# Second feed-forward product begun without its residual, another order in the first quad, and the last weight splits on VectorE

## The chip, the cores and the metric

One core of a Trainium2 chip runs the whole program once. The metric is the device time of one execution in microseconds. The kernel before took 1949.84 us as the median of three runs (1946.95 to 1949.94). The profile is of one more execution, of 1947.49 us, whose span from the first to the last instruction is 1945.7 us.

TensorE multiplies (PE in the profile; PEld is its weight loading), VectorE is DVE, ScalarE is ACT, GpSimd is POOL. Transfers are issued from the queue of SyncE (SP) or of ScalarE (ACTq).

## The reference, cut to what matters

One layer of an encoder on 1024 new frames and 64 frames of a running stream, model width 1024, all in float32. Only its last two lines are touched here:

```
x1 = layer_norm(ALPHA * x + merged @ w_out, ln1_g, ln1_b)
ff = jnp.square(jax.nn.relu(x1 @ w_ff1)) @ w_ff2          # w_ff1: 1024 x 4096, w_ff2: 4096 x 1024
x2 = layer_norm(ALPHA * x1 + ff, ln2_g, ln2_b)
```

`ALPHA * x1` is the residual of the second product.

## The kernel before

**Precision.** Each float32 factor is split in a high and a low part, both stored as float32r: ScalarE copies (`split`, L357), VectorE subtracts (L360). A product is three matmuls, high by high, high by low, low by high (`mm3`, L349, L352, L353).

**Layout.** Activations lie transposed, features on the partitions and the 1088 frames along the free axis, up to the last stage. Until the feed-forward part they lie in three chunks of 384, 384 and 320 frames (`CHUNKS`).

**Units.** Up to the feed-forward part, work comes as units: 128 columns of a weight against one chunk each, 24 matmuls a chunk (`product`, `unit`). A queue of jobs sets their order. Each job loads the weight piece after the next (`wload`, two buffers `wr`) and splits the next one (`wsplit`, two buffers `wh`/`wl`). Work on VectorE and ScalarE for the next stage is written as generators that go one step on at each unit (`BG`, `slot`).

**Opening of the feed-forward part** (`open_ff`, `first_units`). The last 512 of the 4096 hidden columns are four units with relu and square after them (`post_h`), stored in `hidD`. They bridge the layer norm of the third chunk: u0, u1 and u2 run on chunk 0 and 1 while chunk 2 is normalised, then u0 and u1 on chunk 2, then the rest of u2, then u3 on chunks 0, 1, 2. Meanwhile `spill_x1` writes `x1` (high, low and whole: `x1Dh`, `x1Dl`, `y1D`) to memory, and `x1_sums` computes sums of quarters of `x1` (t1 to t4), over the first two chunks in two pieces of 192 frames, each with two tiles of the two `wr` buffers. The third chunk's sums come in `ff_first`.

**Quads.** The other 3584 hidden columns are done as 2 by 2 blocks with seven instead of eight products (`stream`). A quad is seven steps P1 to P7, over 256 columns of the result and all 1088 frames. The order of the steps is P6, P1, P7, P5, P4, P2, P3, where P6, P7, P4 are of the quad before; the first quad has P1, P5, P2, P3 alone. `USES` says which weight sum and which operand sum a step needs, `BANK` which PSUM tile it adds to: P1, P6, P7, P4 add up in bank tile a (two buffers), P5 and P3 in b, P2 in c. After each step `done` reads the banks, so P6 of a quad has to wait until P1 has been read. `between` is called after each step and issues what comes next.

- `ff_first`: 14 quads of 24 matmuls a step. Operands `xb` are loaded from `x1Dh` and `x1Dl` into the buffers that the chunks of `x1` held, once these are done with; weights come through one `raw` buffer (`load_raw`), their sums are split in `produce` (`wv`). `done` makes the hidden layer and its sums and stores them in `hvD`, 14 writes a quad.
- `ff_second`: 7 blocks of 4 quads, 12 matmuls a step. Operands `hv` of even blocks come into the big buffers that `xb` held (`load_even`, into `BIG`), of odd blocks into a pool of their own (`load_odd`). Weights: `load_w`, two buffers `wr`, and `split_w` into parts a, b, c (`wac`, `wb`); `next_w(q + 3)` after P4 of quad q. Results add up in SBUF in four tiles `YF[0..3]` (`yf`), one for each quad of a block. At the start of `ff_second` they are loaded from `y1D`, two on ACTq and two on SP, so the residual is in them from the start; the first accumulation in block 0 multiplies by `ALPHA` (L1307), the others add (L1309). Each step's result goes to one half of a tile, 128x544.
- Pools on one stack take the place of the closed ones: in `ff_second` first `wr2`, then `wvb` (for `wb`), then `y2p` (for `yf`), then `hvp1`. A new tile waits for the last use of what lay there.

**The end.** The 512 hidden columns of the four units are the last factor of the second product. In block 6 `last_weight(k)` (after P2 of quads 24 to 27) loads and splits 128 rows of `w_ff2`, and `last_hidden(k)` 128 rows of `hidD`; their low parts are computed on GpSimd (`low=G`). `last_ff2` then goes through nine tiles of 128 frames: `turn` transposes `yf` (8 transposes, read by ScalarE), `last_products` multiplies, VectorE adds (L1418), and a layer norm follows. From the second tile on all PSUM tiles come from one pool of eight banks.

`tc.issue_after(x)` keeps what its block traces behind instruction x on x's engine.

Of the kernel before, what the change touches and what calls it, by code (L numbers as in the profile page):

```python
# [9 lines left out]
F32 = mybir.dt.float32  # L10
# [7 lines left out]
D = 1024  # L18
# [3 lines left out]
P = 128  # L22
# [29 lines left out]
def hybrid_layer(ctx, tc, x_prompt, x_sample, cache_conv, state_C, state_n, state_m, w_in, b_gate,  # L52
# [50 lines left out]
    def J(ap, fn, kind="w"):  # L103
        jobs.append((ap, fn, kind, stage[0]))
# [823 lines left out]
    def x1_sums():  # L928
        tv = pools["tv"] = pool("tv", 1, stack=ff1)
        for nm in ("t1", "t2", "t3", "t4"):  # L930
            XV[nm] = [tv.tile([P, 4, HT2], F32R, tag=nm + e, name="x" + nm + e) for e in "hl"]

        for o in (0, 192):
            yield from sums(o, 192, 0, o, 1, o)

    def sums(a, n, ca, oa, cb, ob):
        b11, b21 = (Y2[ca][:, kh:KT:2, oa:oa + n] for kh in range(2))
        b12, b22 = (Y2[cb][:, kh:KT:2, ob:ob + n] for kh in range(2))
        z = [wpool.tile([P, KT * P], F32, tag="wr", name="xs")[:, :4 * n].rearrange("p (k t) -> p k t", t=n) for _ in range(2)]

        def keep(nm, src):
            split(*(t[:, :, a:a + n] for t in XV[nm]), src)
        V.tensor_tensor(z[0], b11, b12, ALU.subtract)
        keep("t1", z[0])
        yield
        V.scalar_tensor_tensor(z[1], z[0], -1.0, b22, ALU.mult, ALU.subtract)
        keep("t2", z[1])
        yield
        V.tensor_tensor(z[0], b22, b12, ALU.subtract)
        keep("t3", z[0])  # L950
        V.scalar_tensor_tensor(z[1], z[1], -1.0, b21, ALU.mult, ALU.subtract)
        keep("t4", z[1])
        yield

    def first_units(u, hi, lo):
        post = post_h(u)
        unit(hi, lo, post, (0,))
        held.append((hi, lo, post))
        if u == 1:
            third = 2 + next(i for i, p in enumerate(pieces) if p[3] == 1)  # L960
            w3 = pools["rawp"].tile([P, 2 * KT * P], F32R, tag="raw", name="w3")
            h3, l3 = w3[:, 0:KT * P], w3[:, KT * P:]
            split(h3, l3, raws[third])
            his[third] = tuple(t.rearrange("p (k n) -> p k n", n=P) for t in (h3, l3))
            early[0] = product(*his[third], 0)
            for h in held:
                unit(*h, (1,))
            early[1] = product(*his[third], 1)
            drain("misc")
            for ci in range(3):  # L970
                spill_x1(ci)
            BG["misc"].append(x1_sums())
            step("misc")
            for h in held:
                unit(*h, (2,))

    N(open_ff)
    for u in range(4):
        c0 = (4 * KT - 4 + u) * P
        if u < 2:  # L980
            J(wcols(w_ff1[0], c0), lambda hi, lo, u=u: first_units(u, hi, lo), "f" if u else "w")
        else:
            add_unit(w_ff1[0], c0, post_h(u))

    def stream(n, weight, operand, nk, done, between=None):

        bank = {}

        def run(q, nm):
            an, bn = USES[nm]  # L990
            bk = BANK[nm]
            if nm in ("P1", "P2", "P5"):
                bank[q, bk] = pools["psy" + bk].tile([P, 2, 512], F32, tag=bk, name="y" + bk)
            ps = bank[q, bk]
            for sg in range(2):
                for k in range(nk):
                    bh, bl = operand(q, bn, k, slice(sg * HB, (sg + 1) * HB))
                    mm3(ps[:, sg, :HB], *weight(q, an, k), bh, bl, nm in ("P1", "P2", "P5") and k == 0, k == nk - 1, more=True)
            done(q, nm, {k: bank.get((q, k)) for k in "abc"})

        for q in range(n + 1):
            for nm in ("P6", "P1", "P7", "P5", "P4", "P2", "P3"):
                old = nm in ("P6", "P7", "P4")
                if 0 <= q - old < n:
                    run(q - old, nm)
                    if between:
                        between(q - old, nm)
# [12 lines left out]
    def ff_first():  # L1020
# [26 lines left out]
        def produce():  # L1047
            for q in range(NQ):
# [3 lines left out]
                def item(nm, src):  # L1052
# [6 lines left out]
                    slot_of[q, nm] = (hi, lo)  # L1059
                    made[0] += 1  # L1060
                item("a11", c[0, 0])
                V.tensor_tensor(c[0, 0], c[0, 0], c[1, 0], ALU.add)
                yield
                V.tensor_tensor(c[1, 0], c[1, 0], c[1, 1], ALU.add)
                item("s1", c[1, 0])
                yield
                item("a12", c[0, 1])
                yield
# [183 lines left out]

    def ff_second():
        wr2 = pools["wr2"] = pool("wr2", 2)
        wvb = pool("wvb", 3)
        yp = pool("y2p")
        odd = ExitStack()
        hvp1 = pool("hvp1", 1, stack=odd)
        banks = ExitStack()
# [39 lines left out]
        def done(q, nm, bk):  # L1299
            blk, jp = divmod(q, 4)  # L1300
            for m, b, mh, th in (("P1", "a", 0, 0), ("P5", "b", 1, 1), ("P2", "c", 0, 0), ("P6", "a", 0, 1), ("P6", "b", 0, 1),
                                 ("P7", "a", 1, 1), ("P4", "a", 1, 0)):
                if m == nm:
                    y = halves(YF[jp][:, mh, th * HT2:(th + 1) * HT2])
                    op = ALU.subtract if mh else ALU.add
                    if blk == 0 and (nm, b) in (("P1", "a"), ("P5", "b"), ("P6", "a"), ("P4", "a")):
                        V.scalar_tensor_tensor(y, y, ALPHA, cols2(bk[b]), ALU.mult, op)  # L1307
                    else:
                        V.tensor_tensor(y, y, cols2(bk[b]), op)  # L1309

        def between(q, nm):
            if (q, nm) == (1, "P5"):
                next_w(2)
            if nm == "P4":
                next_w(q + 3)
            blk, n = q // 4, len(steps)
            steps.append(nm)
# [12 lines left out]
            if nm == "P2" and blk == 6:  # L1330
                last_weight(q % 4)
            if q == nq - 1 and nm in ("P5", "P2"):
                k, pp = (2, ph) if nm == "P5" else (3, pl)
                t = pp.tile([P, 3072], F32R, tag="p", name="hid")
                last_hidden(k, t[:, 0:TW], t[:, TW:2 * TW])
# [4 lines left out]

        steps, lead = [], []

        def load_y(j, eng):
            eng.dma_start(YF[j], y1D[j * 2 * P:(j + 1) * 2 * P, :].rearrange("(b p) t -> p b t", p=P))
        load_y(0, S)
        load_w(2, S)
        load_y(1, S)
        load_w(3, S)
        load_y(2, nc.sync)
        load_y(3, nc.sync)  # L1350
        stream(nq, weight, operand, 2, done, between)
        last_ff2(YF, lead[0], banks)

    WH, WL = [], []

    def last_hidden(k, hi, lo):
        raw = pools["la"].tile([P, T], F32, tag="hidr", name="hidr")
        nc.sync.dma_start(raw, hidD[k * P:(k + 1) * P, :])
        for x in (hi, lo):
            G.memset(x[:, T:].bitcast(F32), 0.0)  # L1360
        split(hi[:, :T], lo[:, :T], raw, low=G)
        HID[k] = (hi, lo)

    def last_weight(k):
        la = pools["la"]
        raw = pools["wr2"].tile([P, KT * P], F32, tag="wr", name="wr")
        nc.sync.dma_start(raw, w_ff2[0, (28 + k) * P:(29 + k) * P, :])
        WH.append(la.tile([P, D], F32R, name=f"w2h{k}"))
        WL.append(la.tile([P, D], F32R, name=f"w2l{k}"))
        split(WH[k], WL[k], raw, low=G)  # L1370
        if k < 2:
            last_hidden(k, la.tile([P, TW], F32R, name=f"hid{k}h"), la.tile([P, TW], F32R, name=f"hid{k}l"))

    def last_products(i, hf, p, ks):
        hs = slice(hf * 512, hf * 512 + 512)
# [5 lines left out]
    def last_ff2(YF, lead, banks):  # L1381
# [6 lines left out]
        ps = [None]  # L1388

        def turn(i, banks=None):  # L1390
            n = tile_len(i)
            yt = ytp[:, i % 3 * D:(i % 3 + 1) * D]
            for kh in range(2):
                p = banks[:, kh] if banks is not None else ps[0].tile([P, 512], F32, tag="m", name="pt")
                for k in range(4):
                    j = 4 * kh + k
                    TE.transpose(p[:n, k * P:(k + 1) * P], YF[j // 2][:, j % 2, i * P:i * P + n], ident)
                S.activation(yt[:n, kh * 512:(kh + 1) * 512], p[:n], AF.Copy)
            return yt

        prev = None
        for i in range(NT):
# [6 lines left out]
            for hf in range(2):  # L1409
                hs = slice(hf * 512, hf * 512 + 512)  # L1410
                if i:
                    p = ps[0].tile([P, 512], F32, tag="m", name="po")
# [5 lines left out]
                V.tensor_tensor(y[:, hs], p[:n], y[:, hs], ALU.add)  # L1418
            if i == 0:
                banks.close()  # L1420
                ps[0] = pool("pse", 8, space=PSUM)
                nxt = turn(1)
            stats = ln_stats([y[:, 0:512], y[:, 512:1024]], n)
            if prev:
# [94 lines left out]
```

## Time and profile before

| | |
|---|---|
| median of three runs | 1949.84 us |
| the profiled execution's own time | 1947.49 us |
| its span | 1945.7 us |
| PE busy | 1888.8 us, 97% |
| DVE busy | 1411.8 us, 73% |
| ACT busy | 714.4 us, 37% |
| POOL busy | 144.4 us, 7% |
| mean granted clock of TensorE | 0.990 |

The page cuts the span in 40 slices of 48.6 us. Rows of stretches ("windows") give, for each stretch, its length, then busy time and number of instructions for PE, PEld, DVE, ACT, POOL, then the granted clock, the busy share of the DMA engines and GB/s. A row of the timeline gives start, duration, engine, line, operation, out<-in; in brackets how long the engine sat idle before and what ended it.

### The profile page before, as it was taken

How to read it: one execution, taken by the hardware profiler on the slowest of the kernel's cores; microseconds unless marked ns; L12 is line 12 of the kernel's file. 1: busy time of each engine (PE TensorE's matmuls, PEld its weight loads, DVE VectorE, ACT ScalarE, POOL GpSimd, SP SyncE). 2: the span in 40 equal slices, each digit the busy share in tenths (PEclk: the TensorE clock that was granted, in tenths of full speed). 3: DMA queues.
4: the chain of work that ended last, by engine and by line, in shares of the span. 5: the costliest groups of instructions: out<-in, count | busy, mean ns of one | idle time of the engine just before them, and what ended most of it. 6: DMA issues, size and time to landing. Idle time of an engine off the chain costs nothing.

```text
span 1945.7 us, 31671 instructions
## 1 busy us (share of the span) xinstructions
PE 1888.8 (97%) x12732; PEld 1867.9 (96%) x12732; DVE 1411.8 (73%) x2280; ACT 714.4 (37%) x1269; POOL 144.4 (7%) x237
## 2 busy tenths in 40 slices
PE   8999999999999999999999999899999959999998
PEld 7999999999999999999999999899999959999986
DVE  4957876787678867877774557687777747888856
ACT  4323322332233223323452215676666611212223
POOL 1112210001000100000000000000000000000134
PEclk9999999999999999999999999999999979999999
DMA  4121311122112211225334316856666897676322
GB/s 143 52 78 54 125 51 53 53 72 57 56 33 65 75 56 44 61 88 191 111 107 144 92 36 227 296 213 230 243 235 235 326 337 268 243 269 237 119 78 82
DMA packets 231350, 269.31 MB, mean 138 GB/s; under 512 B 13599, under 2 KB 170767, under 8 KB 231203
## 3 DMA queue, kind: packets, MB, share of 16 engines
q1 hardware_dynamic: 227299, 261.78, 40.0%
q10 hardware_dynamic: 3904, 5.51, 0.8%
q8 instruction: 100, 1.64, 0.3%
q14 instruction: 47, 0.39, 0.1%
HBM read 172.35 MB, written 94.82 MB: 137 GB/s over the span
## 4 chain that ended last, share of the span: by engine, by line
PE 91%; DVE 4%; DMA 3%; ACT 1%; issue 1%; POOL 0%; SPq 0%; ACTq 0%; DVEq 0%; POOLq 0%
PE g L349 18%; PE g L352 18%; PE g L353 18%; PE ya L349 5%; PE ya L352 5%; PE ya L353 5%; PE yb L352 3%; PE yb L353 3%; PE yb L349 3%; PE yc L352 1%; PE yc L353 1%; PE yc L349 1%; PE m L353 1%; PE m L349 1%; PE m L352 1%; PE po L353 1%
## 5 line engine op out<-in xcount | busy, mean ns | idle before, releaser
L349 PE MATMUL g<-xh,wh 128*128 128x384 f32 (+1 forms) x1920 | 634.4, 330 | 0.4 <-ACT xh L180 0.4
L352 PE MATMUL g<-xl,wh 128*128 128x384 f32 (+1 forms) x1920 | 628.3, 327 | 0.9 <-DVE xl L181 0.9
L353 PE MATMUL g<-xh,wl 128*128 128x384 f32 (+1 forms) x1920 | 628.3, 327 | 0.0
L352 PEld LDWEIGHTS g<-xl,wh 128*128 128x128 f32 x1920 | 360.7, 188 | 1.3 <-DVE xl L181 1.2
L349 PEld LDWEIGHTS g<-xh,wh 128*128 128x128 f32 x1920 | 360.6, 188 | 1.1 <-ACT xh L180 0.6
L353 PEld LDWEIGHTS g<-xh,wl 128*128 128x128 f32 x1920 | 360.3, 188 | 0.1
L593 DVE SCALAR_TENSOR_TENSOR acc<-glu,vecs,acc 128x1118 f32<-128x1118 f32 x240 | 332.5, 1385 | 3.6
L357 ACT ACTIVATE wh<-wr 128x1024 fp32r<-128x1024 f32 x83 | 87.9, 1059 | 189.3 <-PE g L352 167.9
L360 DVE TENSOR_TENSOR wl<-wr,wh 128x1024 fp32r<-128x1024 f32 x83 | 103.8, 1250 | 64.0 <-ACT wh L357 63.1
L349 PE MATMUL ya<-hv,wac 128*128 128x272 f32 x336 | 98.3, 293 | 27.9 <-DVE yf L1307 24.6
L357 ACT ACTIVATE wac<-wr 128x512 fp32r<-128x512 f32 (+1 forms) x52 | 44.0, 847 | 175.5 <-PE ya L353 90.7
L353 PE MATMUL ya<-hv,wac 128*128 128x272 f32 x336 | 98.1, 292 | 0.0
L352 PE MATMUL ya<-hv,wac 128*128 128x272 f32 x336 | 97.6, 291 | 0.0
L1309 DVE TENSOR_TENSOR yf<-yf,ya 128x544 f32<-128x544 f32 x100 | 71.7, 718 | 32.2 <-PE ya L353 32.2
L349 PEld LDWEIGHTS ya<-hv,wac 128*128 128x128 f32 x336 | 64.9, 193 | 28.6 <-DVE yf L1307 25.1
L360 DVE TENSOR_TENSOR wv<-raw,wv 128x512 fp32r<-128x512 f32 x84 | 56.5, 686 | 23.3 <-ACT wv L357 22.9
L360 DVE TENSOR_TENSOR wac<-wr,wac 128x512 fp32r<-128x512 f32 (+1 forms) x52 | 49.9, 959 | 30.7 <-ACT wac L357 30.6
L357 ACT ACTIVATE wv<-raw 128x512 fp32r<-128x512 f32 x84 | 51.2, 623 | 48.0 <-DMA raw<-in_w_ff_dram 40.0
L353 PE MATMUL yb<-hv,wac 128*128 128x272 f32 x224 | 65.7, 293 | 0.0
L349 PE MATMUL yb<-hv,wac 128*128 128x272 f32 x224 | 65.6, 293 | 0.0
L352 PE MATMUL yb<-hv,wac 128*128 128x272 f32 x224 | 65.6, 293 | 0.0
L352 PEld LDWEIGHTS ya<-hv,wac 128*128 128x128 f32 x336 | 64.4, 192 | 0.0
(410 smaller groups left out, 4318.2 us busy)
## 6 DMA issues: line engine op xcount, KB each, us to landing
hv<-hvD SPq DMA_DIRECT2D x90, 544.0 KB
wr<-in_w_in_dram SPq DMA_DIRECT2D x64, 512.0 KB
hvD<-zh SPq DMA_DIRECT2D x98, 272.0 KB
wr<-in_w_ff_dram SPq DMA_DIRECT2D x32, 512.0 KB
raw<-in_w_ff_dram SPq DMA_DIRECT2D x15, 1024.0 KB
hvD<-r SPq DMA_DIRECT2D x56, 272.0 KB
hvD<-t SPq DMA_DIRECT2D x42, 272.0 KB
hv<-hvD SPq DMA_DIRECT2D x16, 272.0 KB
```

The costliest lines, as they stand in the source:

```text
L349: first = TE.matmul(out, lh, rh, start=start, stop=False, skip_group_check=more)
L352: TE.matmul(out, lh, rl, start=False, stop=False, skip_group_check=more)
L353: TE.matmul(out, ll, rh, start=False, stop=stop, skip_group_check=more)
L357: a = S.activation(hi, src, AF.Copy)
L360: low.tensor_tensor(lo, src, hi.bitcast(F32), ALU.subtract)
L593: V.scalar_tensor_tensor(acc, glu[:, j:j + AC], vecs[:, c, j:j + 1], acc, ALU.mult, ALU.add))
L1309: V.tensor_tensor(y, y, cols2(bk[b]), op)
```

## The change

1. `x1_sums` goes over the first two chunks in three pieces of 128 frames. A piece that narrow takes one `wr` buffer for its two tiles.
2. `first_units`: all four units are handled in it. u0 on chunk 2, then the split of u3, u1 on chunk 2, u3 on chunks 0 and 1, u2 on chunk 2, u3 on chunk 2.
3. `stream`: the first quad's order becomes P1, P2, P5, P3, in both products. `produce` makes the weight part a12 of the first quad before s1.
4. `ff_second` no longer loads `yf`. In block 0 the first write to each half is a ScalarE copy (scale 1 or -1), the rest add on VectorE. `residual(q)`, after P3 of quads 4 to 9, 12 to 17 and 20 to 23, loads one of 16 pieces of `y1D` (128x544) into a spare part of `BIG[4]` or `BIG[5]`; the call after it adds ALPHA times the piece on VectorE. `y2p` is opened before `wvb`.
5. Weights: `next_w(2)` comes after P4 of quad 0, behind its evacuations, and `next_w(3)` after P3 of quad 1.
6. The last splits: loads and splits are separate, with a timetable `LAST` over quads 24 to 27; the low parts are on VectorE; `hidr` has two buffers.
7. `last_ff2`: two PSUM pools of four banks, for odd and even tiles, instead of one of eight.

```diff
-        for o in (0, 192):
-            yield from sums(o, 192, 0, o, 1, o)
+        for o in range(0, CN, P):
+            yield from sums(o, P, 0, o, 1, o)
...
-            early[0] = product(*his[third], 0)
+            ps3 = [product(*his[third], 0)]
             for h in held:
                 unit(*h, (1,))
-            early[1] = product(*his[third], 1)
+            ps3.append(product(*his[third], 1))
...
-            for h in held:
-                unit(*h, (2,))
+            unit(*held[0], (2,))
+            wsplit(third + 1)
+            for ci in range(2):
+                post_h(2)(ci, *CHUNKS[ci], ps3[ci])
+            unit(*held[1], (2,))
+            unit(*his[third + 1], post_h(3), (0, 1))
+            unit(*his[third], post_h(2), (2,))
+            unit(*his[third + 1], post_h(3), (2,))
...
-            for nm in ("P6", "P1", "P7", "P5", "P4", "P2", "P3"):
+            for nm in ("P6", "P1", "P7", "P5", "P4", "P2", "P3") if q else ("P1", "P2", "P5", "P3"):
...
         wr2 = pools["wr2"] = pool("wr2", 2)
+        yp = pool("y2p")
         wvb = pool("wvb", 3)
-        yp = pool("y2p")
...
                     if blk == 0 and (nm, b) in (("P1", "a"), ("P5", "b"), ("P6", "a"), ("P4", "a")):
-                        V.scalar_tensor_tensor(y, y, ALPHA, cols2(bk[b]), ALU.mult, op)
+                        tail["s"] = S.activation(y, cols2(bk[b]), AF.Copy, scale=-1.0 if mh else 1.0)
                     else:
-                        V.tensor_tensor(y, y, cols2(bk[b]), op)
+                        tail["v"] = V.tensor_tensor(y, y, cols2(bk[b]), ALU.subtract if mh else ALU.add)
+
+        def residual(q):
+            life, i = divmod(q - 4, 8)
+            if i - 1 in rest:
+                (j, mh, th), t = rest.pop(i - 1)
+                y = YF[j][:, mh, th * HT2:(th + 1) * HT2]
+                V.scalar_tensor_tensor(y, t, ALPHA, y, ALU.mult, ALU.add)
+            n = 6 * life + i
+            if i < 6 and n < 16:
+                j, mh, th = n // 4, n // 2 % 2, n % 2
+                t = BIG[4 + i % 2][:, 4 * HT2:5 * HT2].bitcast(F32)
+                r = (2 * j + mh) * P
+                nc.sync.dma_start(t, y1D[r:r + P, th * HT2:(th + 1) * HT2])
+                rest[i] = ((j, mh, th), t)
 
         def between(q, nm):
-            if (q, nm) == (1, "P5"):
-                next_w(2)
-            if nm == "P4":
+            if (q, nm) == (0, "P4"):
+                with tc.issue_after(tail["s"].ins), tc.issue_after(tail["v"].ins):
+                    next_w(2)
+            elif (q, nm) == (1, "P3"):
+                next_w(3)
+            elif nm == "P4":
                 next_w(q + 3)
...
-        load_y(0, S)
         load_w(2, S)
-        load_y(1, S)
         load_w(3, S)
-        load_y(2, nc.sync)
-        load_y(3, nc.sync)
...
-        split(hi[:, :T], lo[:, :T], raw, low=G)
+        split(hi[:, :T], lo[:, :T], lastr["h", k])
...
-        split(WH[k], WL[k], raw, low=G)
+        split(WH[k], WL[k], lastr["w", k])
+
+    LAST = {(24, "P2"): ((hidden_load, 0), (hidden_load, 1)), (25, "P1"): ((weight_load, 0),),
+            (25, "P2"): ((hidden_split, 0), (hidden_load, 2), (weight_load, 1)),
+            (26, "P1"): ((weight_split, 0), (weight_load, 2)), (26, "P5"): ((hidden_split, 1), (hidden_load, 3)),
+            (26, "P2"): ((weight_split, 1), (weight_load, 3)), (27, "P1"): ((weight_split, 2),),
+            (27, "P5"): ((hidden_split, 2),), (27, "P2"): ((hidden_split, 3),), (27, "P3"): ((weight_split, 3),)}
...
-                ps[0] = pool("pse", 8, space=PSUM)
+                ps.extend(pool(f"pse{e}", 4, space=PSUM) for e in range(2))
```

More of the change, by code (lines that the diff above doesn't have):

```diff
@@ L938, in sums @@
         b12, b22 = (Y2[cb][:, kh:KT:2, ob:ob + n] for kh in range(2))
-        z = [wpool.tile([P, KT * P], F32, tag="wr", name="xs")[:, :4 * n].rearrange("p (k t) -> p k t", t=n) for _ in range(2)]
+        z = []
+        for i in range(2):
+            if i == 0 or n > P:
+                t = wpool.tile([P, KT * P], F32, tag="wr", name="xs")
+            j = 4 * n * (i if n <= P else 0)
+            z.append(t[:, j:j + 4 * n].rearrange("p (k t) -> p k t", t=n))
         def keep(nm, src):
@@ L979, in hybrid_layer @@
         c0 = (4 * KT - 4 + u) * P
[L980 to L983, printed above, removed]
+        J(wcols(w_ff1[0], c0), lambda hi, lo, u=u: first_units(u, hi, lo) if u < 2 else None, "f" if u else "w")
     def stream(n, weight, operand, nk, done, between=None):
@@ L1061, in produce @@
                 item("a11", c[0, 0])
+                if q == 0:
+                    yield
+                    item("a12", c[0, 1])
                 V.tensor_tensor(c[0, 0], c[0, 0], c[1, 0], ALU.add)
@@ L1066, in produce @@
                 yield
-                item("a12", c[0, 1])
-                yield
+                if q:
+                    item("a12", c[0, 1])
+                    yield
                 tmp = pools["tmpw"].tile([P, 4 * P], F32, tag="t", name="tw") if q else ztile("tw").bitcast(F32)[:, :4 * P]
@@ L1304, in done @@
                     y = halves(YF[jp][:, mh, th * HT2:(th + 1) * HT2])
-                    op = ALU.subtract if mh else ALU.add
                     if blk == 0 and (nm, b) in (("P1", "a"), ("P5", "b"), ("P6", "a"), ("P4", "a")):
-                        V.scalar_tensor_tensor(y, y, ALPHA, cols2(bk[b]), ALU.mult, op)
+                        tail["s"] = S.activation(y, cols2(bk[b]), AF.Copy, scale=-1.0 if mh else 1.0)
                     else:
-                        V.tensor_tensor(y, y, cols2(bk[b]), op)
-        def between(q, nm):
-            if (q, nm) == (1, "P5"):
-                next_w(2)
-            if nm == "P4":
+                        tail["v"] = V.tensor_tensor(y, y, cols2(bk[b]), ALU.subtract if mh else ALU.add)
+        rest, tail = {}, {}
+        def residual(q):
[11 more added lines that the diff above has]
+                rest[i] = ((j, mh, th), t)
+        def between(q, nm):
+            if (q, nm) == (0, "P4"):
[4 more added lines that the diff above has]
+            elif nm == "P4":
                 next_w(q + 3)
@@ L1329, in between @@
                 load_even(blk + 2)
[L1330 to L1335, printed above, removed]
+            if nm == "P3" and q >= 4:
+                residual(q)
+            for what, k in LAST.get((q, nm), ()):
+                what(k)
             if q == nq - 1 and nm in ("P6", "P7"):
@@ L1341, in ff_second @@
         steps, lead = [], []
-        def load_y(j, eng):
-            eng.dma_start(YF[j], y1D[j * 2 * P:(j + 1) * 2 * P, :].rearrange("(b p) t -> p b t", p=P))
-        load_y(0, S)
         load_w(2, S)
-        load_y(1, S)
         load_w(3, S)
-        load_y(2, nc.sync)
-        load_y(3, nc.sync)
         stream(nq, weight, operand, 2, done, between)
@@ L1354, in hybrid_layer, with hidden_load, hidden_split, weight_load @@
     WH, WL = [], []
-    def last_hidden(k, hi, lo):
-        raw = pools["la"].tile([P, T], F32, tag="hidr", name="hidr")
-        nc.sync.dma_start(raw, hidD[k * P:(k + 1) * P, :])
+    lastr = {}
+    def hidden_load(k):
+        lastr["h", k] = pools["la"].tile([P, T], F32, tag=f"hidr{k % 2}", name="hidr")
+        nc.sync.dma_start(lastr["h", k], hidD[k * P:(k + 1) * P, :])
+    def hidden_split(k):
+        if k < 2:
+            hi, lo = (pools["la"].tile([P, TW], F32R, name=f"hid{k}{e}") for e in "hl")
+        else:
+            t = (ph, pl)[k % 2].tile([P, 3072], F32R, tag="p", name="hid")
+            hi, lo = t[:, 0:TW], t[:, TW:2 * TW]
         for x in (hi, lo):
             G.memset(x[:, T:].bitcast(F32), 0.0)
-        split(hi[:, :T], lo[:, :T], raw, low=G)
+        split(hi[:, :T], lo[:, :T], lastr["h", k])
         HID[k] = (hi, lo)
[L1364 to L1369, printed above, removed]
-        split(WH[k], WL[k], raw, low=G)
-        if k < 2:
-            last_hidden(k, la.tile([P, TW], F32R, name=f"hid{k}h"), la.tile([P, TW], F32R, name=f"hid{k}l"))
+    def weight_load(k):
+        lastr["w", k] = pools["wr2"].tile([P, KT * P], F32, tag="wr", name="wr")
+        nc.sync.dma_start(lastr["w", k], w_ff2[0, (28 + k) * P:(29 + k) * P, :])
+    def weight_split(k):
+        WH.append(pools["la"].tile([P, D], F32R, name=f"w2h{k}"))
+        WL.append(pools["la"].tile([P, D], F32R, name=f"w2l{k}"))
+        split(WH[k], WL[k], lastr["w", k])
[4 more added lines that the diff above has]
+            (27, "P5"): ((hidden_split, 2),), (27, "P2"): ((hidden_split, 3),), (27, "P3"): ((weight_split, 3),)}
     def last_products(i, hf, p, ks):
@@ L1387, in last_ff2 @@
         nc.sync.dma_start(pools["b2"], ln2_b[0:1, :].partition_broadcast(P))
-        ps = [None]
+        ps = []
         def turn(i, banks=None):
@@ L1393, in turn @@
             for kh in range(2):
-                p = banks[:, kh] if banks is not None else ps[0].tile([P, 512], F32, tag="m", name="pt")
+                p = banks[:, kh] if banks is not None else ps[i % 2].tile([P, 512], F32, tag="m", name="pt")
                 for k in range(4):
@@ L1411, in last_ff2 @@
                 if i:
-                    p = ps[0].tile([P, 512], F32, tag="m", name="po")
+                    p = ps[i % 2].tile([P, 512], F32, tag="m", name="po")
                     last_products(i, hf, p, range(4))
```

## The prediction

> **What bounds the kernel now.** I read the page first. TensorE is busy 97% of the span, so the change can only win in the slices where PE falls below 9, and it loses wherever a steady slice gets a hole.
>
> ```profile
> span 1945.7 us, 31671 instructions
> PE 1888.8 (97%) x12732; PEld 1867.9 (96%) x12732; DVE 1411.8 (73%) x2280; ACT 714.4 (37%) x1269; POOL 144.4 (7%) x237
> ...
> PE   8999999999999999999999999899999959999998
> ```
>
> The low slices are 25 (about 1216 to 1265 us, the opening of the feed-forward part), 32 (1556 to 1605, where the second product begins), and both ends. Next, the waits of PE, longest in total first:
>
> ```profile
> PE ya L349 <- DVE yf L1307: 24.6, 2, 18.0
> ...
> PE ya L349 <- DMA xb<-x1Dh: 3.5, 1, 3.5
> PE ya L349 <- DVE yf L1309: 3.3, 1, 3.3
> PE ya L352 <- DMA xb<-x1Dl: 1.5, 1, 1.5
> PE pt L1397 <- DVE big L1418: 1.4, 1, 1.4
> PE yb L349 <- ACT wv L357: 1.3, 1, 1.3
> PE ya L349 <- ACT wv L357: 1.2, 1, 1.2
> ```
>
> L1307 is the first accumulation of block 0, which needs the residual; two waits on it make 24.6 us. The xb and wv rows are the opening, L1309 the last block, pt the start of the end stage. Waits do not show the slow clock after a pause, so I take what each place costs from stretches of 10 us. A steady stretch of the quads has 82 matmuls in 10 us (0.122 us each).
>
> ```profile
> 1240.00:1250.00 10.00, 3.78 (x19) 3.02 (x19) 9.81 (x15) 7.65 (x14) 0.00 (x0) 0.82 1.06 401
> 1250.00:1260.00 10.00, 10.00 (x71) 10.00 (x70) 5.03 (x8) 3.14 (x5) 0.00 (x0) 0.84 1.04 400
> 1260.00:1270.00 10.00, 8.77 (x70) 8.55 (x70) 4.00 (x7) 5.83 (x10) 0.00 (x0) 1.00 0.34 121
> ...
> 1550.00:1560.00 10.00, 5.13 (x41) 4.90 (x40) 6.50 (x10) 4.34 (x8) 0.00 (x0) 1.00 1.04 389
> 1560.00:1570.00 10.00, 0.00 (x0) 0.00 (x0) 2.27 (x4) 1.29 (x2) 0.00 (x0) 0.52 0.93 319
> 1570.00:1580.00 10.00, 6.42 (x34) 6.21 (x34) 3.42 (x7) 1.78 (x3) 0.00 (x0) 0.63 1.02 388
> 1580.00:1590.00 10.00, 3.83 (x17) 3.83 (x18) 3.92 (x6) 0.63 (x1) 0.00 (x0) 0.71 1.04 406
> 1590.00:1600.00 10.00, 10.00 (x78) 10.00 (x78) 8.28 (x15) 1.97 (x3) 0.00 (x0) 0.95 0.57 206
> 1600.00:1610.00 10.00, 10.00 (x82) 10.00 (x82) 7.72 (x14) 1.12 (x3) 0.00 (x0) 1.00 0.84 306
> ...
> 1850.00:1860.00 10.00, 6.71 (x41) 6.53 (x40) 5.27 (x9) 4.12 (x4) 5.00 (x3) 0.83 0.44 155
> ```
>
> - Start of the second product: 41 + 0 + 34 + 17 + 78 = 170 matmuls where 410 fit; 240 are missing, 240 x 0.122 = **29.3 us**. Of these 24.6 are the two waits, the other 4.7 the clock of 0.52 to 0.71.
> - Opening: 160 matmuls where about 243 fit; 83 x 0.122 = **10.1 us**.
> - Last block: 41 of 82, **5.0 us**, of which 3.3 is the wait.
> - Start of the end stage: **1.4 us**.
>
> **The change part by part.**
>
> *The residual (the large term).* Removed from the start are four loads of 1088 KB and the wait of L1307 for them. The chain of waits and two rows of the timeline show what else stands there:
>
> ```profile
> 1552.63 8.65 DMA wr<-in_w_ff_dram
> ...
> 1572.62 10.91 DMA yf<-y1D
> ```
>
> ```profile
> 1543.27 8.29 SPq L1226 DMA_DIRECT2D hv<-hvD  x8
> ...
> 1554.84 0.29 PE L353 MATMUL ya<-hv,wac 128*128 128x272 f32 x1
> ...
> 1573.13 0.60 PE L349 MATMUL ya<-hv,wac 128*128 128x272 f32 x1 [18.00 <-DVE yf L1307]
> ...
> 1541.58 0.61 ACT L1146 ACTIVATE T<-yb 128x544 f32<-128x544 f32 x1
> ...
> 1561.30 0.63 ACT L357 ACTIVATE wac<-wr 128x512 fp32r<-128x512 f32 x1 [6.42 <-DMA wr<-in_w_ff_dram]
> ```
>
> When PE stops (1554.84), P1, P2 and P5 of quad 0 and P1 of quad 1 are done: 24 matmuls of bank a and 12 of b since P4 of the first product. With the residual gone, P1's bank is read by a ScalarE copy; a copy of that shape out of PSUM took 0.61 us. Then come P3, P6, P7 of quad 0 and P5 of quad 1, at 12 x 0.122 = 1.5 us a step, and P4 of quad 0 at 1555.0 + 4 x 1.5 = 1561.0. It needs the last of the eight operand loads, issued by 1551.6. The weight load issued after them (1552.63) landed at 1561.28, so they had landed by about then: P4 is late by some 0.3 us, and the steps ahead of it have their loads earlier in the same queue. Next late is quad 2's weight: landed at 1561.28, queued behind P4's copy (change 5), part a split by 0.63 us on ScalarE and as much on VectorE, about 1564.5; P1 of quad 2 comes at 1567. Part c needs some 5 us more of VectorE and ScalarE, and P5 of quad 2 comes at 1570: about 1 us late. `yf` now lies where t1 and t2 lay, which steps P5 and P6 of the last quad have read by then, and not on tiles still being written out. I leave 2.5 us for these, so the gain is 29.3 - 2.5 = **26.8 us**. Bounds: 29.3 if nothing is left; 11 if transfers are the true limit (rivals).
>
> *The residual's 16 pieces.* 16 more VectorE instructions; the nearest row has 0.718 us, 11.5 us in all, and 16 loads of 272 KB on SP. They fall in the steady part:
>
> ```profile
> 1600.00:1640.00 40.00, 40.00 (x321) 40.00 (x321) 32.36 (x54) 7.43 (x11) 0.00 (x0) 1.00 0.92 342
> ...
> L1309 DVE TENSOR_TENSOR yf<-yf,ya 128x544 f32<-128x544 f32 x78 | 55.9, 718 | 15.7 <-PE ya L353 15.7
> ...
> L360 DVE TENSOR_TENSOR wac<-wr,wac 128x1024 fp32r<-128x1024 f32 x21 | 25.7, 1226 | 21.5 <-ACT wac L357 21.4
> ```
>
> VectorE is busy 32.4 of 40 us, so a quad of 7 x 1.5 = 10.5 us leaves 2.0 us. In each quad it idles 21.5 / 21 = 1.0 us just before the split of part c, waiting for ScalarE, and P3's `between` is there: a piece of 0.7 us fits. Its cover is that idle time; without it a piece costs at most 0.7 us of PE, 11.5 in all. Queued behind the piece are the split of part c and the reading of P6, for which P7 waits. A piece has a quad to land; the first of each series is issued behind eight operand loads:
>
> ```profile
> 1621.47 9.11 SPq L1226 DMA_DIRECT2D hv<-hvD  x8
> ...
> 1640.00:1645.00 5.00, 5.00 (x42) 5.00 (x41) 3.47 (x6) 1.05 (x2) 0.00 (x0) 1.00 0.36 114
> ...
> 1635.46 0.72 DVE L1309 TENSOR_TENSOR yf<-yf,yc 128x544 f32<-128x544 f32 x1
> ```
>
> The transfers thin out only after 1640, and VectorE reaches the add behind this reading of P2, at about 1637: up to 3 us late, three times. I take **1.0 us** lost, between 0 and 11.5.
>
> How the cut in pieces bears on the transfers is told by a stretch in which only such pieces were issued:
>
> ```profile
> DMA packets 1920, 3.76 MB, mean 376 GB/s; under 512 B 197, under 2 KB 197, under 8 KB 1919
> ```
>
> At 376 GB/s a piece takes 0.74 us of the engines. The Trainium skill ("DMA: Bandwidth & Descriptors", section "Measured (HBM→SBUF, 128 partitions, SWDGE, issued from GpSimd)") speaks against the cut: it wants transfers of 1 MiB and more for three quarters of the peak, and has 138 GB/s at 64 KB. By that figure (an estimate from the page) a piece would take 2.0 us, the three late pieces 1.3 us more each, and the sum would be some 4 us worse. The trace disagrees: pieces in a row on one queue ran at 376 GB/s.
>
> *The opening.* Two things become free. First, a sum's second tile no longer waits for the weight buffer that u3 holds. Before, the first sum (L943) ran at 1198.5 and the second not until u3's split was over:
>
> ```profile
> 1198.50 0.96 DVE L943 TENSOR_TENSOR xs<-y,y 128x768 f32<-128x768 f32 x1
> ...
> 1227.91 0.96 DVE L946 SCALAR_TENSOR_TENSOR xs<-xs,y 128x768 f32<-128x768 f32 x1
> ```
>
> The stretch 1240 to 1250 has VectorE at 9.81 of 10, and some of these sums can go ahead of it. Second, the buffers of chunks 0 and 1 are free one product of chunk 2 (3.5 us) earlier. Against it: the first `raw` weight load waits for the third unit, which now ends one product (3.5 us) before the opening's end instead of three (11.7 us). And transfers fill this stretch (1.06 and 1.04 of the engines, 400 GB/s), with the same bytes as before, so the second quad's weight cannot land much sooner. I take a gain of **1.5 us**, between -6 (`raw` late by the 8.2 us, less what other steps cover) and +7.5 (all four waits gone). 24 sums of 512 columns in place of 16 of 768 are 1.2 us more of VectorE, inside this.
>
> *The last splits.* On GpSimd they held VectorE up:
>
> ```profile
> 1846.19 2.54 POOL L360 TENSOR_TENSOR hid1l<-hidr,hid1h 128x1088 fp32r<-128x1088 f32 x1 [0.76 <-ACT hid1h L357]
> ...
> 1843.61 2.10 DVE L1242 TENSOR_TENSOR wr<-wr 128x256 f32<-128x256 f32 x1
> 1846.45 2.57 DVE L360 TENSOR_TENSOR wb<-wr,wb 128x256 fp32r<-128x256 f32 x1
> ...
> L1242 DVE TENSOR_TENSOR wr<-wr 128x256 f32<-128x256 f32 x21 | 8.8, 418 | 0.0
> ```
>
> Two instructions that elsewhere take 0.42 us took 2.10 and 2.57, and the second ended as GpSimd's split did (at 1848.7 and 1849.0): 3.8 us late on VectorE, and the 3.3 us wait of PE. Now eight splits of about 1.25 us (row of 1226 ns) go to VectorE, one before quad 26 and seven after; the weight splits of 4 us a quad end there, so it has room. A split of 1.25 us ahead of P6's or P7's reading (0.7 us) outlasts the 1.5 us step that covers it by 0.4: I leave 1.0 us. Gain 5.0 - 1.0 = **4.0 us**, between 0 and 5.0.
>
> *PSUM pools.* The second tile's transposes no longer take the bank that L1418 reads: **1.4 us**, between 0 and 1.4.
>
> **Sum**, against the profiled execution (1947.49 us): 26.8 - 1.0 + 1.5 + 4.0 + 1.4 = 32.7, which gives 1914.8 us. The profiled execution lies 2.35 us below the median of the three runs (1949.84), inside their scatter of 3 us. I predict 1915 us.
>
> **The rivals.**
>
> 1. *Transfers take the residual's place.* The engines moved 319 to 406 GB/s through all of 1550 to 1590. For: the operand loads, stores and weights that crowd there stay, and VectorE's wait may become PE's wait for operands. Then the gain is only what the four loads took, 4.46 MB at 400 GB/s = 11 us instead of 26.8: 1931. Against: block 0's operands were there by 1561. Chance 0.13.
> 2. *Only the residual pays.* The opening loses 3 us on the late `raw` load and the last splits gain nothing on a VectorE that is full: 26.8 - 1 - 3 + 0 + 1.4 = 24.2, 1923. For: 9.81 of 10 at the opening. Chance 0.15.
> 3. *The start stays blocked behind weights,* that is, the change does not do what it says: ScalarE, which now reads the banks, sits at quad 2's split until 1561.28, as before (a wait of 6.4 us there). P1's copy would end at 1562 instead of 1555: 7 us, 1922. Against: the edit orders the split behind the copies. Chance 0.07.
> 4. *Slower: VectorE in order behind late pieces.* Each of the 16 adds holds up whatever is behind it while its piece is under way. It decides once a piece is late by more than the gain 33.7 / 16 = 2.1 us plus the 1 us of idle time, 3.1 us on the mean; at 5 us each it is 16 x 4 = 64 lost, 1947.5 + 64 - 33.7 = 1978. Against: 13 of 16 have a whole quad without a burst. Chance 0.04.
>
> **How the numbers follow.** The forecast, 1906 to 1920 by its own terms, has 0.61. All bounds at their good end are 29.3 + 0 + 7.5 + 5.0 + 1.4 = 43.2, so 1904; I reach to 1905. The high end takes in rivals 2 and 3 and, at 1931, rival 1: 1905 to 1931. Under 0.2% (4 us) is no change for a measurement of this kernel: cases 1 to 3 and the forecast are all beyond it, so faster has 0.95, no change 0.01, slower 0.04.
>
> **What would show it.** No wait of PE on `yf` at the second product's start; a granted clock of 1.00 there, 390 to 410 matmuls in its first 50 us. VectorE at 9.2 to 9.4 of 10.5 us a quad where pieces are added, and no wait on `y1D` over 3 us. GpSimd without L360 in the last block, and no VectorE instruction of 2 us. No wait of pt on L1418. The opening's gaps (xb, wv) still some 8 us. Wrong would be: PE waiting for `hv` or `wac` for over 5 us after the first product, or holes in the steady quads.

## The result, and the profile after

The changed kernel takes 1926.78 us (median of 4 runs, 1926.2 to 1931.17) against 1949.89 us (4 runs, 1946.95 to 1951.41): a ratio of 0.9888, 95% interval 0.9869 to 0.9907, or 23 us. The forecast was 1915: the direction is right, the time lies inside the range, and the gain is 12 us short of the forecast.

The page of the changed kernel, engines and slices of the span:

```profile
span 1929.1 us, 31716 instructions
PE 1891.8 (98%) x12732; PEld 1869.8 (97%) x12732; DVE 1411.5 (73%) x2296; ACT 724.1 (38%) x1289; POOL 126.0 (7%) x229
...
PE   7999999999999999999999999899999989999998
```

Slice 32, a 5 before, is now an 8: most of the hole at the second product's start is closed, not all. What is left stands in the waits of PE of the same execution:

```profile
PE ya L349 <- ACT wv L357: 6.5, 1, 6.5
PE ya L349 <- ACT yf L1318: 6.2, 1, 6.2
...
PE ya L349 <- DVE r L1161: 2.1, 1, 2.1
```

The two waits on L1307 (24.6 us together), L1309 and L1418 are gone. In the opening the waits on `xb` and `wv` (3.5, 1.5, 1.3 and 1.2 us) have become one of 6.5 us on `wv`. And there is a wait that no term of the forecast had: 6.2 us on `yf` L1318, ScalarE's copy of the first accumulations.

The stretches of 10 us of the changed kernel (columns as in the prediction):

```profile
1550.00:1560.00 10.00, 8.89 (x56) 8.68 (x57) 8.50 (x16) 6.06 (x12) 0.00 (x0) 0.83 0.94 330
1560.00:1570.00 10.00, 4.21 (x34) 3.99 (x32) 5.64 (x9) 4.26 (x9) 0.00 (x0) 0.96 0.99 372
1570.00:1580.00 10.00, 9.54 (x54) 9.35 (x55) 2.73 (x4) 2.06 (x4) 0.00 (x0) 0.70 0.95 349
1580.00:1590.00 10.00, 10.00 (x80) 9.85 (x80) 7.48 (x16) 5.50 (x10) 0.00 (x0) 1.00 1.03 392
...
1840.00:1850.00 10.00, 10.00 (x83) 10.00 (x82) 8.62 (x12) 3.52 (x4) 0.00 (x0) 1.00 0.47 162
1850.00:1860.00 10.00, 10.00 (x82) 10.00 (x81) 8.22 (x10) 2.27 (x3) 0.47 (x4) 1.00 0.02 5
```

Around the second product's start 56 + 34 + 54 + 80 matmuls stand where 328 fit: 104 missing, 12.7 us, where the forecast left 2.5. The last block has no hole any more, and GpSimd no L360 in it.

This execution was the longest of the four, and a second one, of the same kernel (the run "again" below, 1927.82 us), shows why whole times are a blunt measure here. The table is counted out from the traces: A is 400 matmuls ahead of the first product, B its 168th matmul, D the 336th, E the 2016th and F the last matmul of the second product. Up to A the work is the same in every kernel.

```
us             start-A      A-B      B-D      D-E     E-F   F-end     span
before         1176.89    96.50   346.87   210.21   49.87   65.31  1945.66
after          1180.43    97.20   331.93   211.32   44.95   63.26  1929.10
after, again   1178.78    96.31   330.95   211.38   45.06   63.27  1925.76
```

Up to A the executions of all kernels of this case differ by up to 3.9 us (1176.51 to 1180.43), with the same work in them. Behind it A-B repeats to about 1 us and B-D only to 2.7 us: it took 329.2 to 331.9 us in the changed kernel's two executions and in "gps", "nopieces" and "onepool" below, whose work is the same up to D. The later stages repeat to 0.3 us where nothing in them was changed. So the terms are read from the stages: before to "again" A-B -0.2, B-D -15.9, D-E +1.2, E-F -4.8, F-end -2.0, in sum -21.8 us; B-D lies between -14.9 and -17.7 over those five.

### The profile page after: what moved, and what is told of

It reads as the page before. It is cut to its first block, busy times and chain, and to the rows that moved or that the text cites. A ratio compares the mean times of both kernels' runs of the same rounds, so it can differ in the third digit from the quotient of the medians.

```text
span 1929.1 us, 31716 instructions
## 1 busy us (share of the span) xinstructions
PE 1891.8 (98%) x12732; PEld 1869.8 (97%) x12732; DVE 1411.5 (73%) x2296; ACT 724.1 (38%) x1289; POOL 126.0 (7%) x229
## 4 chain that ended last, share of the span: by engine, by line
PE 88%; DVE 6%; DMA 4%; issue 1%; ACT 1%; POOL 0%; SPq 0%; DVEq 0%; ACTq 0%; POOLq 0%
PE g L349 18%; PE g L352 18%; PE g L353 18%; PE ya L349 5%; PE ya L353 5%; PE ya L352 5%; PE yb L349 2%; PE yb L353 2%; PE yb L352 2%; DMA raw<-in_w_ff_dram 2%; PE yc L349 1%; PE yc L352 1%; PE yc L353 1%; PE m L349 1%; PE m L353 1%
## 5 line engine op out<-in xcount | busy, mean ns | idle before, releaser
L360 DVE TENSOR_TENSOR wl<-wr,wh 128x1024 fp32r<-128x1024 f32 x83 | 103.5, 1246 | 63.9 <-ACT wh L357 63.0
L360 DVE TENSOR_TENSOR wv<-raw,wv 128x512 fp32r<-128x512 f32 x84 | 56.5, 688 | 34.3 <-ACT wv L357 33.9
L360 DVE TENSOR_TENSOR wac<-wr,wac 128x512 fp32r<-128x512 f32 (+1 forms) x52 | 49.8, 958 | 21.6 <-ACT wac L357 21.5
```

The lines of the kernel that those rows point to most:

```text
L360: low.tensor_tensor(lo, src, hi.bitcast(F32), ALU.subtract)
```

## The experiments

**The changed kernel once more.** No edit.

> The changed kernel itself once more, to tell what belongs to it from what belongs to its one profiled execution, in which the transfers of 1529 to 1547 us lagged on some engines (the 16 parts of one load landed over 4 us, before over 0.6). Expected by the theory that ScalarE is held at the start of the second product by a tile that is still being written out: 1926 us, and again one wait of PE of 5 to 7 us on ACT yf L1318, with the last high part of the first product (zh<-t) waiting on DMA hvD for 4 to 6 us just before it. By the rival that this was a whim of one execution: the wait on L1318 is under 2 us and the time some 4 us lower than the profiled one. The idle time of VectorE of 4.1 us at the end of the first product (before the reading of bank c) is expected to shrink to 1 to 2 us if it came from the lag alone.

Measured: 1927.25 us, ratio 0.988 (0.9865 to 0.9895). PE's wait on L1318 is 9.7 us here, longer than in the first execution, and VectorE's idle time ahead of the reading of bank c shrinks from 4.1 to 1.2 us. In the seven other kernels that keep the tile in question it is 9.0 to 9.6 us. So the hold belongs to the change, and the long lag of the transfers to that execution: there it put 4 us more ahead of the start and took 3.5 us from the hold. The stretches of this execution, then ScalarE's timeline (start, duration, in brackets the idle time and what ended it), then the chain of work that ended last:

```profile
1550.00:1560.00 10.00, 7.36 (x59) 7.14 (x58) 8.58 (x13) 6.58 (x11) 0.00 (x0) 1.00 1.04 408
1560.00:1570.00 10.00, 2.98 (x13) 2.96 (x14) 1.36 (x2) 2.19 (x4) 0.00 (x0) 0.61 0.89 336
1570.00:1580.00 10.00, 10.00 (x71) 9.81 (x71) 2.43 (x4) 2.98 (x6) 0.00 (x0) 0.88 0.97 335
```

```profile
1556.46 0.64 ACT L1138 ACTIVATE zh<-r 128x544 fp32r<-128x544 f32 x1
1565.80 0.66 ACT L1138 ACTIVATE zh<-t 128x544 fp32r<-128x544 f32 x1 [8.70 <-DMA hvD<-r]
1566.36 0.61 ACT L1318 ACTIVATE yf<-ya 128x544 f32<-128x544 f32 x1
```

```profile
1548.55 6.21 DMA hv<-hvD
...
1556.73 8.98 DMA hvD<-r
1565.80 0.66 ACT zh L1138
1566.46 0.52 ACT yf L1318
1567.02 0.59 PE ya L349
```

The last high part of the first product, t4's, is to go to a `z` tile that an earlier store still reads. That store, issued at 1556.73 after ten operand loads and two weight loads, took 9 us to land. P1's copy stands behind this one instruction in ScalarE's order, and PE behind the copy. SP's queue had been held up itself. By the trace's semaphore events eight semaphores take turns for the transfers, and in this stretch an issue comes only once the transfer that had its semaphore before has landed: the store was issued 0.06 us after the operand load of 1548.55 had landed (1556.67).

**That tile elsewhere** ("freehigh"): t4's high part of the last quad goes to a place of `t3`, which P7 had read.

```diff
-            Z[nm + "h"] = ztile("zh")
+            Z[nm + "h"] = XV["t3"][0][:, 0, :] if q == NQ - 1 and nm == "t4" else ztile("zh")
```

> The changed kernel, with one tile elsewhere: the high part of t4 of the last quad goes to a place of the operand t3, which was read two steps earlier, and not to a z tile that has to be written out first. Theory (ScalarE in order behind that tile): zh<-t follows its neighbour at once, P1's copy of quad 0 ends some 5 us sooner, PE's wait on L1318 falls from 6.5 us to 1.5 or less, the slow clock after it goes too; 5 to 7 us faster than the changed kernel, some 1920. Rival (the transfers set this stretch): PE waits for hv or wac instead, two or three steps later, and the gain is under 2 us.

Measured: 1930.9 us, ratio 0.9902 (0.9887 to 0.9917), 3.7 us slower than "again"; B-D is 334.3 us. The hold went as the theory said, and a longer one came. ScalarE, the stretches, SP's queue and PE's waits:

```profile
1556.52 0.66 ACT L1138 ACTIVATE xt3h<-t 128x544 fp32r<-128x544 f32 x1 [0.28 <-DVE t L1181]
1557.08 0.60 ACT L1318 ACTIVATE yf<-ya 128x544 f32<-128x544 f32 x1
...
1593.07 0.63 ACT L357 ACTIVATE wac<-wr 128x512 fp32r<-128x512 f32 x1 [15.08 <-DMA wr<-in_w_ff_dram]
...
1593.91 1.12 ACT L1318 ACTIVATE yf<-ya 128x544 f32<-128x544 f32 x2
```

```profile
1560.00:1570.00 10.00, 10.00 (x81) 9.81 (x80) 3.89 (x7) 3.53 (x7) 0.00 (x0) 1.00 0.95 356
1570.00:1580.00 10.00, 10.00 (x81) 9.86 (x80) 7.18 (x14) 4.51 (x6) 0.00 (x0) 1.00 0.86 312
1580.00:1590.00 10.00, 2.71 (x22) 2.49 (x20) 0.00 (x0) 0.00 (x0) 0.00 (x0) 0.89 1.03 405
1590.00:1600.00 10.00, 5.43 (x31) 5.43 (x32) 5.49 (x10) 4.14 (x7) 0.00 (x0) 0.60 0.73 274
```

```profile
1573.12 8.32 SPq L1300 DMA_DIRECT2D hv<-hvD  x11
1582.38 3.63 SPq L1279 DMA_DIRECT2D wr<-in_w_ff_dram  x2
...
PE ya L349 <- ACT yf L1318: 13.1, 2, 11.9
```

The stretches from 1560 to 1580 are full. Then quad 4's weight (L1279) is issued behind 11 operand loads of block 1 (L1300), at 1582.38, and lands at 1593.05. ScalarE waits 15 us for it, and two copies of bank a (1593.91) stand behind the split in its order; PE, which needs that bank, stands from 1582.7 to 1594.6. So PE waits again for a copy and not for an operand, some 11 us before quad 4's own first step would have been due (in the next kernel it begins at 1594.6, and mark A lies 1.2 us later there). The weight's buffer had been free from about 1574.3, when quad 2's last split ended; what made it late was its place on SP, among transfers that ran at 405 GB/s: it was issued 0.06 us after the operand load of 1574.56, which had its semaphore before, had landed (1582.32).

**Both holds away** ("freelate"): as above, and block 1's operand loads are to be issued behind the weights of quads 4 and 5.

```diff
+                tail["w"] = eng.dma_start(rw[q], w_ff2...)
...
-                i = (n % 28 - 3) // 2
-                if (n % 28 - 3) % 2 == 0 and i < 12:
-                    load_odd(blk + 1, i)
+                i = n - 11 if blk == 0 else (n % 28 - 3) // 2
+                if (blk == 0 and i >= 0 or blk and (n % 28 - 3) % 2 == 0) and i < 12:
+                    with tc.issue_after(tail["w"].ins) if blk == 0 else ExitStack():
+                        load_odd(blk + 1, i)
```

> The changed kernel with two edits: the high part of t4 of the last quad in a place of t3 (as in the run before, where the hold at the start went and a wait of 11.9 us for quad 4's weight came 14 us later), and the operand loads of block 1 issued behind the loads of the weights of quads 4 and 5, which they had queued ahead of. Theory (two holds in a row, both by order: first ScalarE behind a tile being stored, then quad 4's weight behind 11 operand loads on SP): both waits fall under 3 us each, the 336th matmul of the second product comes 9 to 12 us sooner than in the repeat of the changed kernel (1606.0), 1915 to 1919 us in all. Rival (the transfers themselves, which run at some 400 GB/s from 1530 to 1600, are the limit): the wait moves on to quad 5's weight or to the operands of block 1, and the time stays at 1923 to 1928 us.

Measured: **1918.61 us**, ratio 0.9838 (0.9823 to 0.9852): faster than both kernels, 8.6 us under "again". B-D is 322.8 us against 331.0 there and 346.9 before. Stretches, SP's queue and what waits are left around the start:

```profile
1560.00:1570.00 10.00, 10.00 (x80) 9.81 (x80) 3.10 (x6) 3.16 (x7) 0.00 (x0) 1.00 0.89 335
1570.00:1580.00 10.00, 10.00 (x81) 9.85 (x80) 8.20 (x17) 5.08 (x8) 0.00 (x0) 1.00 0.91 332
1580.00:1590.00 10.00, 9.02 (x70) 8.58 (x69) 5.79 (x11) 4.27 (x7) 0.00 (x0) 1.00 1.05 401
1590.00:1600.00 10.00, 10.00 (x82) 10.00 (x82) 7.09 (x12) 2.62 (x4) 0.00 (x0) 1.00 1.05 402
```

```profile
1575.79 0.37 SPq L1279 DMA_DIRECT2D wr<-in_w_ff_dram  x1
1576.26 2.15 SPq L1300 DMA_DIRECT2D hv<-hvD  x4
...
PE ya L349 <- DMA hv<-hvD: 1.3, 1, 1.3
```

In SP's order two operand loads still stand ahead of quad 4's weight, in place of 11, and four more ahead of quad 5's. The first weight is issued 6.6 us sooner in the span, its split no longer holds the copies up, and the clock stays at 1.00. Transfers ran at 332 to 402 GB/s here and did not hold PE for more than 1.3 us at a time.

**The second edit alone** ("late"): block 1's loads behind the weights, t4's part in a `z` tile as in the changed kernel.

> The changed kernel with only the second of the two edits of the run that took both holds away: the operand loads of block 1 are issued behind the weights of quads 4 and 5, and t4's high part is written to a z tile as in the changed kernel. Theory (two holds in a row, of which the second shows only once the first is gone, since the 9.7 us that PE stands still let quad 4's weight land in time): no gain, within 1 us of the changed kernel (1927), the wait on L1318 still 9 to 10 us. Rival (queueing behind the weights is worth something by itself): 3 to 8 us faster.

Measured: 1925.78 us, ratio 0.9876 (0.9859 to 0.9893). The interval overlaps that of "again", the wait on L1318 is 9.3 us, D-E is 0.5 us longer. Alone it does next to nothing (A-D 426.7 us, 427.3 in "again"). Its B-D of 329.7 us lies among those of the unchanged kernel. Of the two edits the first alone costs 3.7 us, the second alone brings 1.5 us, which is inside the scatter, and both bring 8.6: the second hold shows only where the first is gone.

**The first weight load sooner** ("rawearly"):

```diff
+            unit(*his[third], post_h(2), (2,))
             unit(*his[third + 1], post_h(3), (0, 1))
-            unit(*his[third], post_h(2), (2,))
```

> The changed kernel, with the third unit's product of chunk 2 ahead of the fourth unit's products of chunks 0 and 1, so that the buffer of the first weight load (raw) is free 2 products (some 6.8 us) sooner. Theory (the 6.5 us wait on ACT wv is the late raw load alone): the wait falls to 2 to 3 us, where the operand loads xb, landed at 1245.9 and 1249.2, are last; 2 to 4 us faster. Rival (what is gained on raw is lost on the operands, whose buffers are read one product, 3.4 us, longer): a wait on xb comes in its place, within 1 us of the changed kernel.

Measured: 1927.53 us, ratio 0.9878 (0.9862 to 0.9895); A-B 97.3 us against 96.3. The waits of PE between 1240 and 1260 us:

```profile
PE ya L349 <- DMA xb<-x1Dh: 2.8, 1, 2.8
PE ya L352 <- DMA xb<-x1Dl: 2.8, 1, 2.8
```

A wait of 1.2 us on `wv` is left beside them: 6.8 us in place of 6.4. The rival is right; what is gained on `raw` is lost on the operands. Transfers fill this stretch in "again" too (1.06 and 1.05 of the engines).

**The sums in halves of 192 columns** ("open192"):

```diff
-        for o in range(0, CN, P):
-            yield from sums(o, P, 0, o, 1, o)
+        for o in (0, 192):
+            yield from sums(o, 192, 0, o, 1, o)
```

> The changed kernel with the sums of the operands in two pieces of 192 columns again, on two tiles. The opening as a whole stood within 0.3 us of before (predicted 1.5 us faster). Theory (the smaller pieces go ahead of the splits and are worth something, which the late raw load takes back): 1 to 4 us slower. Rival (the sums were not on the path): within 0.5 us.

Measured: 1926.26 us, ratio 0.9877 (0.9862 to 0.9892); A-B 96.8 us. Within 0.5 us: the sums were not on the path.

**The first quad in its old order** ("oldorder"):

```diff
-            for nm in (...) if q else ("P1", "P2", "P5", "P3"):
+            for nm in (...) if q else ("P1", "P5", "P2", "P3"):
...
-                if q == 0:
-                    yield
-                    item("a12", c[0, 1])
```

> The changed kernel with the first quad of both products in the order P1, P5, P2, P3 again, and the weight a12 split after s1 again. Theory (the new order lets P2, whose operands need no sum, go ahead of P5 in the opening): from the opening's mark (400 matmuls ahead of the first product) to its 168th matmul 1 to 4 us more than the 96.3 us of the changed kernel; the second product's start within 1 us. Rival (raw and the operand loads set the opening, whatever the order): within 0.5 us in both places.

Measured: 1926.83 us, ratio 0.9879 (0.9864 to 0.9894); A-B 96.3 us, as with the new order. B-D is 332.0 against 331.0, inside the 2.7 us to which this stage repeats. The new order brought nothing in the opening.

**The last splits on GpSimd again** ("gps"), loads and places as changed:

```diff
-        split(WH[k], WL[k], lastr["w", k])
+        split(WH[k], WL[k], lastr["w", k], low=G)
```

(and the same for the hidden rows.)

> The changed kernel, with the low parts of the eight last splits back on GpSimd, their loads and places as changed. Theory (VectorE is held while GpSimd splits): VectorE instructions of 2 to 2.6 us beside each of GpSimd's 2.5 us, holes of PE in the last quads, 3 to 8 us slower than the changed kernel (eight splits instead of the two that hurt before). Rival (before, the hole came from all splits falling late, in the last quad, and the earlier loads cured it): within 1 us.

Measured: 1929.77 us, ratio 0.9893 (0.9878 to 0.9908). E-F is 48.3 us against 45.1: 3.3 us. GpSimd's and VectorE's timelines of this kernel:

```profile
1825.90 2.54 POOL L360 TENSOR_TENSOR hid1l<-hidr,hid1h 128x1088 fp32r<-128x1088 f32 x1
1828.40 2.83 POOL L360 TENSOR_TENSOR w2l<-wr,w2h 128x1024 fp32r<-128x1024 f32 x1
...
1826.76 2.24 DVE L360 TENSOR_TENSOR wac<-wr,wac 128x512 fp32r<-128x512 f32 x1
1829.04 2.48 DVE L1253 TENSOR_TENSOR wr<-wr 128x256 f32<-128x256 f32 x1
```

Instructions of 0.69 and 0.42 us end at 1829.0 and 1831.5 with GpSimd's at 1828.4 and 1831.2, as the last block showed before. The Trainium skill ("SBUF — State Buffer", section "SBUF: two separate sides") says that a VectorE instruction with two inputs in SBUF and a GpSimd instruction that reads SBUF contend for a shared pair of ports, under a lock that is held for a whole instruction while the other blocks fully; these rows agree. The theory is right, at the low end of its price: with eight splits on it PE waits 2.0 and 0.8 us.

**Without the residual's pieces** ("nopieces"):

```diff
-            if nm == "P3" and q >= 4:
-                residual(q)
```

> The changed kernel without the 16 residual pieces: their loads and additions are left out, so the residual is missing from the output. Theory (a piece fits into VectorE's idle time but for a little): the steady stretch from the 336th to the 2016th matmul of the second product takes 210.2 us as before instead of 211.4; 1 to 1.5 us faster. Rival (the pieces' price is in the transfers around the block changes): the same stretch is within 0.3 us of 211.4 and the gain, if any, lies elsewhere.

Measured: 1925.25 us, ratio 0.9872 (0.9857 to 0.9887). D-E is 210.4 us against 211.4: 16 pieces cost 1.0 us.

**One PSUM pool at the end** ("onepool"): `ps[0]` for every tile, one pool of 8 banks.

> The changed kernel with one pool of 8 PSUM banks in the end stage. Theory (the second pool alone took the wait of pt away): the end stage, from the last matmul of the second product to the end, takes 65.3 us as before instead of 63.3, and a wait of PE pt of 1.4 us is back; 1.4 to 2 us slower. Rival (the stage gained because VectorE and GpSimd enter it without late splits): within 0.5 us.

Measured: 1927.22 us, ratio 0.9883 (0.9866 to 0.9899). F-end is 64.95 us against 63.27, and the wait is back:

```profile
PE pt L1434 <- DVE big L1455: 1.5, 1, 1.5
```

The stage says 1.7 us; the medians of the whole time, which scatter by more, do not show it.

## Why the prediction was right or wrong, point by point

```
term                         predicted      measured (stage)
start of the second product    -26.8        -15.9   (B-D, -14.9 to -17.7; with both holds away -24.1)
residual's pieces               +1.0        +1.2    (D-E; +1.0 by leaving them out)
opening                         -1.5        -0.2    (A-B)
last splits                     -4.0        -4.8    (E-F; 3.3 of it from GpSimd)
PSUM pools                      -1.4        -2.0    (F-end; 1.7 by undoing it)
sum                            -32.7       -21.8
```

**The term that was mis-sized** is the first: "P1's bank is read by a ScalarE copy", with 2.5 us left for what is late next. The count of 29.3 us lost before was right, and the change did take the residual out of the start. Wrong was the step that made ScalarE free to copy. I followed the operands, the weights and `yf`'s own place, and wrote that `yf` does not lie "on tiles still being written out"; I did not follow the tile of the instruction that stands just ahead of the copy in ScalarE's order. The trace of before holds a hint. Its ScalarE rows, of the kernel before:

```profile
1561.30 0.63 ACT L357 ACTIVATE wac<-wr 128x512 fp32r<-128x512 f32 x1 [6.42 <-DMA wr<-in_w_ff_dram]
...
1563.11 0.66 ACT L1126 ACTIVATE zh<-t 128x544 fp32r<-128x544 f32 x1 [1.18 <-DVE wr L1241]
```

The landings of the stores, read from the trace's semaphore events, are these:

```
                     a store of r issued   its last part landed   zh<-t began
before                     1553.97               1563.02            1563.11
after                      1560.91               1569.16            1569.24
after, again               1556.73               1565.72            1565.80
```

In all three `zh<-t` begins 0.08 to 0.09 us after a store of `r` lands. Before, ScalarE sat until 1561.30 at quad 2's weight, so of the store's wait only 1.18 us was left, and the profile put that down to another instruction. That it was the store there too rests on the 0.09 us and was not tried. The change moved the weight's split behind the copies, ScalarE came to `zh<-t` at 1557.1, and the wait showed in full, 8.70 us. The granted clock was 0.61 in the 10 us in which the pause ended and 0.88 in the next 10, which adds to it.

**The rivals.** Rival 3 had the form: ScalarE blocked, P1's copy late, "7 us", 1922. The copy's lateness is that (it ended at 1567.0 in "again", and at 1557.7 in "freehigh"), the cause another: the edit that orders the split behind the copies did work, and a store took the weight's place. With that rival's 7 us the start would have gained 19.8. Rival 1 (transfers take the residual's place, 11 us gained, 1931) lies on the other side of the 15.9 measured, nearer in the whole time, and its row held: 335 to 408 GB/s in "again" from 1550 to 1580. But "freelate" has the same loads and stores to move and gains 24.1, so the limit was the order behind the full transfers, not their rate. Rival 2 (1923) is refuted in its parts: the last splits paid in full. Rival 4 did not come: the changed kernel has no wait on `y1D`, and the steady stage lost 1.2 us.

**The pieces** cost what was said. By the prediction's estimate from the Trainium skill's size rule ("DMA: Bandwidth & Descriptors", section "Measured (HBM→SBUF, 128 partitions, SWDGE, issued from GpSimd)") it would have been some 4 us more; 1.0 us measured leaves no room for that.

**The opening** was over-valued: the 0.2 us measured are inside the 1 us to which A-B repeats. The sums, given a gain for going ahead, were worth nothing on the path (96.8 against 96.3 us), nor was the new order. That `raw` comes late was foreseen; that undoing it buys nothing, because the operands then come as late, was not priced.

**The last splits and the PSUM pools** brought 0.8 and 0.6 us more than taken. The first is close to its upper bound of 5.0: the reserve of 1.0 us for splits ahead of the reading of P6 was not needed. The second lies above its bound of 1.4, by 0.3 us where it was undone alone.

**What was to show it.** Of the marks named, no wait on `y1D`, no L360 on GpSimd and no slow VectorE instruction in the last block, and no wait of pt on L1418 came true. The first mark named did not: PE waited 6.2 and 9.7 us on `yf`, for the copy instead of the residual. VectorE came a little under its mark (34.3 of 40 us from 1640 to 1680, 9.0 us a quad instead of 9.2 to 9.4), and the opening's gap was 6.5 us instead of some 8. Neither sign of being wrong appeared: no wait of PE on `hv` or `wac` and no hole in the steady quads. The clock of 1.00 and the 390 to 410 matmuls in the first 50 us did not come true either: 306 stand in the rows of the changed kernel from 1550 to 1600, at a clock down to 0.70. "Freelate" keeps 1.00 from 1550 to 1600 and has 377 there.

## What to carry to other kernels

When a wait is to be removed, or a bank's reading moved to another engine, list what that engine has ahead of the reading in its order, with the buffer or the transfer that each of those instructions needs: here twice a copy of 0.6 us stood behind one that waited 9 to 15 us for a transfer, and the first of these had been hidden behind another wait before the change. Where transfers run full, look at the order in which they are issued before calling their rate the limit. And read a small change by stages between marks of equal work, since here the untouched first 1177 us alone scattered by 3.9 us.

## What the runs showed of the hardware that was not expected

In the profiled execution of the changed kernel one weight load of 1024 KB, issued at 1529.05, landed its 16 parts between 1533.64 and 1537.37 us, 3.7 us apart; the same load before took 0.6 us from the first to the last (1528.85 to 1529.47). The loads and stores issued after it, up to 1548.24, landed over 3 to 5 us each, and VectorE idled 4.1 us until 1546.69, just after the store issued at 1537.43 had landed (1546.61). In "again" the parts of such transfers lay 0.6 to 2.6 us apart there, in "oldorder" up to 3.2. What held some of the engines in that execution stays open.
